# A hybrid SSM and attention encoder in fp32 on one core: another order of the first loads, zeros on TensorE, later lambda loads, four last pieces

## Chip, core and metric

The kernel runs on one core of one Trainium2 chip. The metric is the time of one execution on the device in microseconds; lower is better. Three runs of the kernel before took 1010.69 us in the median, from 1009.72 to 1019.44.

## What is computed

A residual stream x of 256 tokens by 2048 features passes a LayerNorm and then two layers. All is fp32.

```python
def reference(x, ...):
    x = layer_norm(x, ln_emb_g, ln_emb_b)
    for l in range(2):
        u, g_ssm, q, k, v, g_attn = split(x @ w_in[l])      # 2048 -> 6 x 1024
        y = u * ssm_d[l] + s5_scan(u, forward) + s5_scan(u, backward)
        y = gelu(y);  y = y * sigmoid(y @ w_glu[l] + b_glu[l]);  y_ssm = y * silu(g_ssm)
        lam = exp(sum(lambda_q1 * lambda_k1)) - exp(sum(lambda_q2 * lambda_k2)) + lambda_init
        o = rms_norm(diff_attention(rotary(q), rotary(k), v, lam), attn_norm_g[l])
        y_attn = o * (1 - lambda_init) * silu(g_attn)
        x = layer_norm(ALPHA * x + concat(y_ssm, y_attn) @ w_out[l], ln_g[l], ln_b[l])
    return x
```

`s5_scan` first makes small tables from `ssm_lam_re`, `ssm_lam_im` and `ssm_log_step` (exponentials, sines, a reciprocal), 64 groups by 64 states in each direction and layer.

## The kernel before

All weights stream through in tiles of 512 x 256, 512 KB each, in the order of the list `jobs`; I number them from 0. `load` (L144) asks for a tile on SP's DMA queue into one of four buffers `raw`. `do_split` (L156) makes two halves of it: ACT casts `raw` to `wh` (L163), DVE subtracts, `wl = raw - wh` (L165). A product of two fp32 numbers then is three matmuls on TensorE (PE), `mm3` (L168): high by high (L169), low by high (L170) and high by low (L171), with x split in the same way into `xh` and `xl`. A weight tile makes 8 x 3 = 24 matmuls of 256 columns. `step` (L863) splits two tiles ahead and loads four more ahead of these, then multiplies and lets `side` run other work.

The first eight weight tiles belong to two output blocks in turn (L889 to 895): for k tiles 0 to 3, then 4 to 7 and so on, one weight tile of each block. So weight tiles 0 to 3 multiply the first half of x's features, 4 to 7 the second half.

x goes through `ln_finish` (L213). It takes the moments of 128 tokens (`moments`, L220), normalises a piece of columns in two DVE passes (`centre` L230, `norm` L236), transposes it on PE into a `ss` bank (`trans`, L243), and makes `xh` by a cast on ACT (L253) and `xl` by a subtraction on DVE (L254). The pieces are k tiles 0-1, 2-3, 4-7, 8-11 and 12-15 (L281); the last two belong to weight tiles 4 to 7. Each normalised piece is also stored to `xres` for the residual addition (L211). The reciprocal root of the variance, `rstd`, is made on POOL in two steps (L224 adds epsilon, L225 is the power). After layer 1 the same function ends the kernel: there the second 128 tokens are done in the pieces of `LAST_PIECES`, and each is stored to the output (L241).

The start (L802 to L828): x is asked for in eight pieces, behind the first four the identity matrix (`cst`, L809) and the norm's rows `gt` and `bt` for the first 512 features (`load_gb`, L198), then the first four weight tiles with the other norm rows between them, then the other constants (L815).

Work beside the large products runs in lanes (`Lane`, `side`), which are generators: each `yield cost, gap` hands back and says after how many weight tiles it wants its next turn. `ssm_tables` (L296) loads its inputs (L303 to 306) and computes the tables in its first turns, `ssm_load` brings B and C and transposes them, `ssm_in` makes the SSM's input, `ssm_scan` scans it on DVE, `ssm_out` is its output. `lam_of` (L659) loads four lambda rows into the tile `on`, computes lambda, and loads `gsc` (L674), the gain of the headwise norm; it stands ahead of the first weight tile of a layer (L887). `on` is also used by the last table copies of `ssm_tables` and by the attention heads.

This order of calls is not the order on the engines. A scheduler (`schedule_with_timeline_sim=True`) simulates the program and writes each engine's instructions in the order in which they come out ready; the chip then works each engine's list strictly in that order. `with after(ins)` forbids it to place an instruction ahead of `ins`. In the program that comes out SP keeps eight DMAs under way: each issue waits until the one eight places ahead of it has landed.

## Time and profile before

| | before |
|---|---|
| median of three runs | 1010.69 us |
| the profiled execution | 1013.52 us |
| its span, first to last instruction | 1011.7 us |
| TensorE matmul (PE) busy | 960.5 us, 95% |
| weight load (PEld) | 928.7 us, 92% |
| VectorE (DVE) | 777.7 us, 77% |
| ScalarE (ACT) | 576.6 us, 57% |
| GpSimd (POOL) | 72.4 us, 7% |
| moved by DMA | 186.15 MB, 184 GB/s in the mean |

The span is what the profile shows from the first instruction to the last; about 2 us of the execution lie around it. Busy times are sums over the whole span, so they say nothing of a single stage. "PEclk" is the clock that TensorE was granted, as a share of its full 2.4 GHz: 1.00 is that, 0.50 is 1.2 GHz.

### The profile page before, as it was taken

What the parts mean: (1) busy time and instruction counts of PE and PEld (TensorE: products, weight loads), DVE (VectorE), ACT (ScalarE), POOL (GpSimd) and SP (SyncE); (2) the same over time, 40 slices, a digit from 0 to 9 for tenths busy, and PEclk for the clock granted to TensorE, in tenths of its full rate; (3) what the DMA queues carried; (4) which work ended last, traced back from release to release, by engine and by line L of the source; (5) the groups of instructions that cost most, each with busy time, mean ns of one, the idle gap of its engine ahead of it and who ended that gap; (6) DMA issues with size and microseconds to landing.
All of it is one profiled execution on the core that took longest, in us unless ns stands there. A gap on an engine that the chain in (4) does not pass through costs nothing.

```text
span 1011.7 us, 24655 instructions
## 1 busy us (share of the span) xinstructions
PE 960.5 (95%) x10304; PEld 928.7 (92%) x10304; DVE 777.7 (77%) x1326; ACT 576.6 (57%) x950; POOL 72.4 (7%) x103
## 2 busy tenths in 40 slices
PE   2899999999999998998889999999999999999995
PEld 2889988999999998998889989999999999999995
DVE  6784799899887696645489699989899759565576
ACT  2446588555575697435244486555556869833540
POOL 1000130110200000000001030010100100000001
PEclk9999999999999999999999999999999999999998
DMA  8897521545565644779974833555545454577883
GB/s 266 244 267 216 184 85 44 167 148 166 164 180 163 195 123 122 240 230 294 262 245 157 239 93 105 168 174 160 166 148 182 150 170 138 177 240 247 298 258 84
DMA packets 201871, 186.15 MB, mean 184 GB/s; under 512 B 38048, under 2 KB 194464, under 8 KB 201760
## 3 DMA queue, kind: packets, MB, share of 16 engines
q1 hardware_dynamic: 201760, 184.57, 60.1%
q8 instruction: 81, 1.33, 0.6%
q14 instruction: 30, 0.25, 0.1%
HBM read 169.21 MB, written 15.34 MB: 182 GB/s over the span
## 4 chain that ended last, share of the span: by engine, by line
PE 70%; DMA 13%; DVE 7%; ACT 4%; SPq 3%; issue 2%; POOL 1%; POOLq 0%; DVEq 0%; ACTq 0%
PE acc L169 19%; PE acc L170 19%; PE acc L171 19%; DMA rpart<-xr 5%; DMA raw<-in_w_out_dram 4%; DVE wl L165 2%; PE ss L502 2%; PE ss L597 2%; DMA raw<-in_w_glu_dram 2%; ACT wh L163 2%; PE tp L474 1%; PE sc L708 1%; PE ss L736 1%; SPq L428 1%; DVE H L236 1%
## 5 line engine op out<-in xcount | busy, mean ns | idle before, releaser
L165 DVE TENSOR_TENSOR wl<-raw,wh 128x1024 fp32r<-128x1024 f32 x266 | 324.7, 1222 | 148.4 <-ACT wh L163 146.6
L163 ACT CAST wh<-raw 128x1024 fp32r<-128x1024 f32 x266 | 278.4, 1050 | 265.7 <-PE acc L170 105.8
L169 PE MATMUL acc<-xh,wh 128*128 128x256 f32 x1280 | 370.7, 290 | 1.1 <-ACT xh L253 0.9
L170 PE MATMUL acc<-xl,wh 128*128 128x256 f32 x1280 | 365.4, 286 | 3.3 <-DVE xl L254 3.2
L171 PE MATMUL acc<-xh,wl 128*128 128x256 f32 x1280 | 364.3, 285 | 0.7 <-DVE wl L165 0.7
L169 PEld LDWEIGHTS acc<-xh,wh 128*128 128x128 f32 x1280 | 245.3, 192 | 6.1 <-ACT xh L253 1.6
L170 PEld LDWEIGHTS acc<-xl,wh 128*128 128x128 f32 x1280 | 245.8, 192 | 5.2 <-DVE xl L254 4.3
L171 PEld LDWEIGHTS acc<-xh,wl 128*128 128x128 f32 x1280 | 245.7, 192 | 1.8 <-DVE wl L165 1.1
L169 PE MATMUL acc<-wh,xh 128*128 128x256 f32 x720 | 206.0, 287 | 4.7 <-ACT wh L163 2.2
L170 PE MATMUL acc<-wl,xh 128*128 128x256 f32 x720 | 205.3, 286 | 2.4 <-DVE wl L165 1.7
L171 PE MATMUL acc<-wh,xl 128*128 128x256 f32 x720 | 204.1, 284 | 0.0
L169 PEld LDWEIGHTS acc<-wh,xh 128*128 128x128 f32 x720 | 138.5, 193 | 5.8 <-ACT wh L163 2.4
L170 PEld LDWEIGHTS acc<-wl,xh 128*128 128x128 f32 x720 | 138.5, 192 | 4.2 <-DVE wl L165 4.1
L171 PEld LDWEIGHTS acc<-wh,xl 128*128 128x128 f32 x720 | 138.4, 192 | 0.0
L552 DVE TENSOR_TENSOR sa<-tab,H 128x256 f32<-128x256 f32 x126 | 53.1, 421 | 2.9 <-ACT H L505 0.7
L459 DVE TENSOR_TENSOR w<-w,x 128x512 f32<-128x512 f32 x64 | 45.5, 711 | 0.8
L718 ACT ACTIVATE e<-sc,mx 128x256 f32<-128x256 f32 x64 | 29.5, 476 | 21.9 <-DVE mx L712 21.8
L555 DVE TENSOR_TENSOR H<-sa 128x128 f32<-128x128 f32 x126 | 36.1, 287 | 2.1
L554 DVE TENSOR_TENSOR sa<-sa,H 128x128 f32<-128x128 f32 x126 | 36.1, 286 | 1.9
L171 PE MATMUL acc<-bh,wl 128*128 128x256 f32 x128 | 36.4, 284 | 0.9 <-DVE wl L165 0.9
L742 POOL TENSOR_SCALAR ms<-ms 128x2 f32<-128x2 f32 x16 | 16.1, 1008 | 286.8 <-ACT on L741 286.8
L505 ACT COPY H<-ss 128x512 f32<-128x512 f32 x32 | 33.9, 1171 | 4.1 <-PE ss L502 4.1
(188 smaller groups left out, 1282.6 us busy)
## 6 DMA issues: line engine op xcount, KB each, us to landing
raw<-in_w_in_dram SPq DMA_DIRECT2D x192, 512.0 KB, 3.7
raw<-in_w_out_dram SPq DMA_DIRECT2D x64, 512.0 KB, 5.5
raw<-in_w_glu_dram SPq DMA_DIRECT2D x16, 512.0 KB, 5.9
xr<-xres SPq DMA_DIRECT2D x16, 256.0 KB, 3.2
rpart<-xr SPq DMA_DIRECT2D x16, 256.0 KB, 5.4
xr<-rpart SPq DMA_DIRECT2D x15, 256.0 KB, 4.4
xres<-H SPq DMA_DIRECT2D x14, 256.0 KB, 3.4
H<-in_x_dram SPq DMA_DIRECT2D x8, 256.0 KB, 5.9
```

The lines of the kernel that those rows point to most:

```text
L163: A.copy(wh, raw)
L165: V.tensor_tensor(wl, raw, wh.bitcast(F32), sub)
L169: PE.matmul(o, lhsT=lh, rhs=rh, start=first, stop=False, skip_group_check=True)
L170: PE.matmul(o, lhsT=lh, rhs=rl, start=False, stop=False, skip_group_check=True)
L171: PE.matmul(o, lhsT=ll, rhs=rh, start=False, stop=last, skip_group_check=True)
L459: V.tensor_tensor(w[:, r], w[:, r], x2, op)
L502: PE.matmul(ps[g2][ds, pr // 2, ri, pr % 2, :], lhsT=w[rows, pr, ds], rhs=u if d == 0 else u[:, ::-1], start=True, stop=True)
L505: A.copy(z.H[:, 2 * o:2 * o + 2, 1:65].rearrange("p q k r g -> p q (r g) k")[:, :, g2::2], ps[g2].rearrange("p q r g k -> p q (r g) k"))
L552: V.tensor_tensor(a.rearrange("p v q r g -> p v q (r g)"), lam, h.unsqueeze(1).to_broadcast([128, 2, 16, 8]), mult)
L554: V.tensor_tensor(a[:, 0], a[:, 0], nx, add)
L555: V.tensor_tensor(nx, a[:, 0], a[:, 1, :, ::-1, :], add)
L718: A.activation(e[:, m, i, :], sc[:, m, i, :], AF.Exp, bias=mx[:, c:c + 1], accum_out=sm[:, c:c + 1])
```

## The change

1. First loads. All of x is asked for, then the first norm rows, then weight tile 0. Weight tile 0's load is held until DVE has taken the statistics of the first 128 tokens (a memset of one element per partition of `raw`, ordered behind them). The other norm rows are ordered behind the newest weight load.
2. Zeros. A tile of zeros is made on POOL, and PE multiplies it ten times (`WARM`), 128 x 128 by 128 x 512, into a bank that is not read, ahead of the first transpose.
3. Start order. The first two splits name what they follow: the casts of weight tiles 0 and 1, and the `wl` behind the `xl` of their piece. The normalisation of a later piece also follows the `xl` before the last one.
4. SSM tables. Their loads are a turn of their own, the computation begins three weight tiles later (`TAB_HOP`), its first steps ordered behind the newest split.
5. Lambda. The loads of lambda and of `gsc` are a function `lam_load` that is called after the SSM input blocks, behind the newest weight load; `lam_of` computes from them after the first V block.
6. Tail. Epsilon is added on DVE, not on POOL. `LAST_PIECES` is (6,5,3,2), not (6,5,5). Each last piece's two stores are issued one from SP, one from ACT.

```diff
-LAST_PIECES = (6,5,5)
+LAST_PIECES = (6,5,3,2)
+WARM = 10
+TAB_HOP = 3
...
+    def load(i, hold=None):
...
+        if hold:
+            with after(hold):
+                V.memset(raw[:, 0, 0:1], 0.0)
...
-        A.copy(wh, raw)
-        with after(behind):
-            V.tensor_tensor(wl, raw, wh.bitcast(F32), sub)
+        with after(behind[0]):
+            newest[2] = A.copy(wh, raw).ins
+        with after(behind[1]):
+            newest[1] = V.tensor_tensor(wl, raw, wh.bitcast(F32), sub).ins
...
-            GP.tensor_scalar(rstd, mv[:, 1:2], EPS, None, add)
+            V.tensor_scalar(rstd, mv[:, 1:2], EPS, None, add)
...
-                for j in range(2):
-                    SY.dma_start(dst[2 * i + j][:, cs], r[64 * j:64 * j + 64, i, cs])
+                for j, eng in enumerate((SY, A)):
+                    eng.dma_start(dst[2 * i + j][:, cs], r[64 * j:64 * j + 64, i, cs])
...
-                with after(last):
+                with after(last), after(los[-2] if ahead < 8 and len(los) > 1 else None):
                     last = norm(i, k0, nk, *m)
...
+        yield 0.0, TAB_HOP
         step = T([128, 2], "p_st")
-        A.activation(step, ls, AF.Exp)
+        with after(newest[2]), after(newest[1]):
+            A.activation(step, ls, AF.Exp)
+        first = newest[1]
...
-    def lam_of(l):
+    def lam_load(l):
         t = T([128, 4, 64], "on")
...
+        gs = T([128, 1], "gsc", 2)
+        with after(newest[0]):
+            for i, src in enumerate((lambda_q1, lambda_k1, lambda_q2, lambda_k2)):
+                SY.dma_start(t[:, i, :], src[l:l + 1, :].to_broadcast([128, 64]))
+            SY.dma_start(gs, attn_norm_g[l].unsqueeze(1))
+        return t, gs
+
+    def lam_of(l, t, gs):
...
-            load_gb(gt, bt, ln_emb_g, ln_emb_b, slice(0, 512))
-    for c in range(RAW_BUFS):
-        load(c)
-        if c < 3:
-            load_gb(gt, bt, ln_emb_g, ln_emb_b, slice(512 * c + 512, 512 * c + 1024))
-    SY.dma_start(cst[:, C_SEL:], consts[:, C_SEL:])
+    load_gb(gt, bt, ln_emb_g, ln_emb_b, slice(0, 512))
+
+    idle = tp_bank([128, 512])
+    for _ in range(WARM):
+        PE.matmul(idle, lhsT=zero[:, 0:128], rhs=zero, start=True, stop=True)
...
+    for c in range(8):
+        seen = ln_stats(r, 0, c, st)
+    for c in range(RAW_BUFS):
+        load(c, hold=seen if c == 0 else None)
+        if c < 3:
+            with after(newest[0]):
+                load_gb(gt, bt, ln_emb_g, ln_emb_b, slice(512 * c + 512, 512 * c + 1024))
+    SY.dma_start(cst[:, C_SEL:], consts[:, C_SEL:])
+    next(ln)
+    for c in range(8):
+        ln_stats(r, 1, c, st)
     for i in range(SPLIT_AHEAD):
         next(ln)
-        do_split(i, behind=box[1][0])
+        do_split(i, behind=box[2] if i else (None, box[2][1]))
...
-        neg, gsc = lam_of(l)
...
+        lam = lam_load(l)
...
+                with after(newest[1]):
+                    neg, gsc = lam_of(l, *lam)
```

What stood in SP's queue behind the first four weight loads, before. `cst` are the constants, `on` the lambda rows, `kx` and `p_ls` the inputs of the SSM tables; the first `raw` is weight tile 4, the second tile 5:

```order
L815 DMA cst<-in_consts_dram 128x595
L662 DMA on<-in_lambda_q_dram 128x64
L662 DMA on<-in_lambda_k_dram 128x64
L662 DMA on<-in_lambda_q_dram 128x64
L662 DMA on<-in_lambda_k_dram 128x64
L150 DMA raw<-in_w_in_dram 128x4x256
L674 DMA gsc<-in_attn_norm_g_dram 128x1
L303 DMA kx<-in_ssm_lam_re_dram 64x2x64
L304 DMA kx<-in_ssm_lam_im_dram 64x2x64
L306 DMA p_ls<-in_ssm_log_step_dram 64x1
L150 DMA raw<-in_w_in_dram 128x4x256
```

In the changed kernel, from the last two table loads before weight tile 4 on; ahead of these stand the constants and the other table loads. The three `raw` of before and after are told apart by place: here the first is tile 4, the second tile 5.

```order
L313 DMA p_ls<-in_ssm_log_step_dram 64x1 x2
L310 DMA kx<-in_ssm_lam_re_dram 64x2x64
L311 DMA kx<-in_ssm_lam_im_dram 64x2x64
L313 DMA p_ls<-in_ssm_log_step_dram 64x1 x2
L155 DMA raw<-in_w_in_dram 128x4x256
L217 DMA xres<-H 128x512
L217 DMA xres<-H 128x256 x2
L217 DMA xres<-H 128x512
L448 DMA dd<-in_ssm_d_dram 16x16x1 x2
L217 DMA xres<-H 128x512
L448 DMA dd<-in_ssm_d_dram 16x16x1 x2
L155 DMA raw<-in_w_in_dram 128x4x256
```

Weight tile 4 stood between the lambda and the table loads; now it stands behind all table loads, and five stores of x and four small loads of `dd` stand between it and tile 5.

On ACT, before, from the cast of weight tile 3 on; `xh_117` is the first half of the features, `xh_141` the second:

```order
L163 CAST wh<-raw 128x1024
L253 CAST xh_117<-ss 128x512
L163 CAST wh<-raw 128x1024
L668 ACTIVATE le_178<-ls_176 128x2
L253 CAST xh_141<-ss 128x512
L308 ACTIVATE p_st<-p_ls 128x2
L163 CAST wh<-raw 128x1024
L253 CAST xh_141<-ss 128x512
L314 ACTIVATE kx<-kx 128x128
```

In the changed kernel, from the casts of weight tiles 1 and 2 on; `xh_131` is the first half, `xh_155` the second:

```order
L169 CAST wh<-raw 128x1024 x2
L260 CAST xh_131<-ss 128x512
L169 CAST wh<-raw 128x1024
L260 CAST xh_131<-ss 128x512
L169 CAST wh<-raw 128x1024 x2
L317 ACTIVATE p_st<-p_ls 128x2
L169 CAST wh<-raw 128x1024
L260 CAST xh_155<-ss 128x512 x2
L326 ACTIVATE kx<-kx 128x128
```

Before, the first cast of the second half stood behind the casts of weight tiles 3 and 4; now the casts of tiles 4, 5 and 6 stand ahead of it.

## Rows read from the trace of the kernel before

**Rows 1.** Stretches: from:to, length, busy of PE, PEld, DVE, ACT, POOL, PEclk, DMA, GB/s

```profile
0.00:20.00 20.00, 1.80 (x6) 1.01 (x6) 10.29 (x24) 3.10 (x4) 3.68 (x12) 1.00 0.91 261
...
40.00:60.00 20.00, 17.46 (x140) 16.65 (x139) 14.83 (x42) 9.91 (x14) 0.00 (x0) 1.00 0.88 261
...
140.00:160.00 20.00, 19.45 (x483) 16.16 (x471) 19.57 (x33) 15.77 (x28) 6.13 (x8) 1.00 0.10 30
```

**Rows 2.** PE's waits, 40 to 50 us: total, times, longest

```profile
PE acc L170 <- DVE xl L254: 2.3, 1, 2.3
```

**Rows 3.** Time line of ACT and DVE: start, busy, instruction, idle before and its releaser

```profile
16.03 1.04 ACT L163 CAST wh<-raw 128x1024 fp32r<-128x1024 f32 x1 [2.44 <-DMA raw<-in_w_in_dram]
...
18.95 1.22 DVE L165 TENSOR_TENSOR wl<-raw,wh 128x1024 fp32r<-128x1024 f32 x1
```

**Rows 4.** Time line of SP's queue: start and length of each DMA issue

```profile
17.24 0.33 SPq L815 DMA_DIRECT2D cst<-in_consts_dram  x1
...
22.98 0.38 SPq L150 DMA_DIRECT2D raw<-in_w_in_dram  x1
```

**Rows 5.** DMA issues at 17.24, from 25.5 to 28.4, and the stores of x

```profile
cst<-in_consts_dram SPq DMA_DIRECT2D x1, 297.5 KB, 8.8
...
raw<-in_w_in_dram SPq DMA_DIRECT2D x1, 512.0 KB, 3.6
...
DMA to landing us min/median/max: 3.2/4.7/5.2
```

**Rows 6.** Time line of PE: first matmuls of weight tiles 4 and 8

```profile
37.04 0.40 PE L169 MATMUL acc<-xh,wh 128*128 128x256 f32 x2
...
52.62 0.39 PE L169 MATMUL acc<-xh,wh 128*128 128x256 f32 x1 [0.18 <-ACT ub L881]
```

**Rows 7.** Time line of DVE from 36.35, and two later instructions

```profile
36.35 0.74 DVE L236 SCALAR_TENSOR_TENSOR H<-H,rstd 128x512 f32<-128x512 f32 x1
37.01 1.21 DVE L165 TENSOR_TENSOR wl<-raw,wh 128x1024 fp32r<-128x1024 f32 x1
38.15 0.68 DVE L254 TENSOR_TENSOR xl<-ss,xh 128x512 fp32r<-128x512 f32 x1
38.75 0.21 DVE L316 TENSOR_SCALAR kx<-kx 128x128 f32<-128x128 f32 x1
...
45.43 0.15 DVE L675 TENSOR_SCALAR gsc<-gsc 128x1 f32<-128x1 f32 x1 [5.00 <-DMA gsc<-in_attn_norm_g_dram]
...
52.26 0.94 DVE L340 RECIPROCAL kx<-kx 128x128 f32<-128x128 f32 x1
```

**Rows 8.** Stretches as in rows 1, a wait of PE, a group of matmuls

```profile
20.24:25.03 4.79, 4.66 (x20) 4.37 (x21) 4.79 (x8) 2.32 (x3) 0.00 (x0) 1.00 0.87 287
...
30.00:35.00 5.00, 5.00 (x44) 5.00 (x44) 5.00 (x8) 2.23 (x5) 0.00 (x0) 1.00 0.86 256
...
390.30:393.70 3.40, 3.40 (x86) 3.28 (x83) 2.37 (x4) 3.31 (x7) 0.00 (x0) 0.50 0.29 77
...
390.05 0.55 PE L597 MATMUL ss<-bh,w 64*64 64x64 f32 x8 [2.88 <-ACT ub L608]
...
L736 PE MATMUL ss<-v,wT 128*128 128x128 f32 x128 | 16.8, 274 | 0.0
```

**Rows 9.** PE's waits from 315 to 325 us

```profile
PE acc L171 <- DVE wl L165: 0.7, 1, 0.7
```

**Rows 10.** Time line of DVE at the end, and the stretch from 1009

```profile
1001.46 1.81 DVE L230 SCALAR_TENSOR_TENSOR H<-H,mv 128x768 f32<-128x768 f32 x2
...
1003.74 1.02 DVE L236 SCALAR_TENSOR_TENSOR H<-H,rstd 128x768 f32<-128x768 f32 x1 [0.47 <-POOL rstd L225]
...
1009.00:1010.00 1.00, 0.00 (x0) 0.00 (x0) 0.00 (x0) 0.00 (x0) 0.00 (x0) 0.50 1.01 261
```

**Rows 11.** The last step of the first layer's scan on DVE, and PE behind it

```profile
341.70 0.29 DVE L555 TENSOR_TENSOR H<-sa 128x128 f32<-128x128 f32 x1
...
349.47 0.69 PE L578 MATMUL tp<-cst,kw 128*64 128x64 f32 x16
```

More of the change, by code (lines that the diff above doesn't have):

```diff
@@ L141 @@
     raws, split = {}, {}
-    newest = [None]
-    def load(i):
+    newest = [None, None, None]
+    def load(i, hold=None):
         if i >= len(jobs):
@@ L154, in load, with do_split @@
         raws[i] = raw
-    def do_split(i, wh=None, wl=None, behind=None):
+    def do_split(i, wh=None, wl=None, behind=(None, None)):
         if i >= len(jobs):
@@ L201, in ln_stats @@
     def ln_stats(r, i, c, st):
-        V.bn_stats(st[:, i, c, :], r[:, i, c * 256:(c + 1) * 256])
+        return V.bn_stats(st[:, i, c, :], r[:, i, c * 256:(c + 1) * 256]).ins
     stores = []
@@ L218, in ln_finish @@
         pool = [None]
+        los = []
         def moments(i):
@@ L252, in trans @@
             h, lo_ = box[0].h[k0 // 8][sl], box[0].l[k0 // 8][sl]
-            A.copy(h, t)
-            V.tensor_tensor(lo_, t, h.bitcast(F32), sub)
+            box[2] = A.copy(h, t).ins, V.tensor_tensor(lo_, t, h.bitcast(F32), sub).ins
+            los.append(box[2][1])
         mv, rstd = moments(0)
@@ L306, in ssm_tables @@
                 SY.dma_start(ls[ps, d:d + 1], ssm_log_step[l, d].unsqueeze(1))
+        yield 0.0, TAB_HOP
         step = T([128, 2], "p_st")
-        A.activation(step, ls, AF.Exp)
+        with after(newest[2]), after(newest[1]):
+            A.activation(step, ls, AF.Exp)
+        first = newest[1]
         for d in range(2):
             dsl = slice(64 * d, 64 * d + 64)
-            V.tensor_scalar(zr[:, dsl], lr[:, dsl], step[:, d:d + 1], None, mult)
-            V.tensor_scalar(zi[:, dsl], li[:, dsl], step[:, d:d + 1], None, mult)
+            with after(first):
+                V.tensor_scalar(zr[:, dsl], lr[:, dsl], step[:, d:d + 1], None, mult)
+            with after(first):
+                V.tensor_scalar(zi[:, dsl], li[:, dsl], step[:, d:d + 1], None, mult)
         mag = t1
@@ L657 @@
     swap = list(range(8, 16)) + list(range(0, 8)) + list(range(16, 32))
-    def lam_of(l):
+    def lam_load(l):
         t = T([128, 4, 64], "on")
-        for i, src in enumerate((lambda_q1, lambda_k1, lambda_q2, lambda_k2)):
-            SY.dma_start(t[:, i, :], src[l:l + 1, :].to_broadcast([128, 64]))
+        gs = T([128, 1], "gsc", 2)
[5 more added lines that the diff above has]
+    def lam_of(l, t, gs):
         tv = t.rearrange("p (m k) d -> p m k d", m=2)
@@ L672, in lam_of @@
         V.scalar_tensor_tensor(neg, e2[:, 1:2], -init, e2[:, 0:1], add, sub)
-        gs = T([128, 1], "gsc", 2)
-        SY.dma_start(gs, attn_norm_g[l].unsqueeze(1))
         V.tensor_scalar(gs, gs, 1.0 - init, None, mult)
@@ L802 @@
     r, gt, bt = ln_tiles()
+    zero = T([128, 512], "e4")
+    GP.memset(zero, 0.0)
     for i in range(2):
@@ L818 @@
     ln = ln_finish(r, gt, bt, st, None, box, 4)
-    for i in range(2):
-        for c in range(8):
-            ln_stats(r, i, c, st)
-        if i == 0:
-            next(ln)
+    for c in range(8):
[9 more added lines that the diff above has]
+        ln_stats(r, 1, c, st)
     for i in range(SPLIT_AHEAD):
         next(ln)
-        do_split(i, behind=box[1][0])
+        do_split(i, behind=box[2] if i else (None, box[2][1]))
         load(RAW_BUFS + i)
```

## The prediction

> **What bounds the kernel now.** I read first the busy time by stretches, then PE's waits, then the queue of SP and the landing of its transfers, then DVE's instructions one by one. Up to about 20 us TensorE (PE) does next to nothing, 1.80 us in twenty; between 40 and 60 it loses another 2.5; from 60 on it loses little, 0.55 in the stretch from 140 to 160, one of the worse ones [rows 1]. So the kernel is bound by PE, and this change can only win what PE idles: the start, one wait at 44 us (2.3 us, for an `xl` that DVE is late with [rows 2]), small waits later, and the tail after PE's last matmul. The start itself is a matter of transfers and DVE: the first weight tile lands at 16.03, where ACT's wait for it ends, and its split is complete at 18.95 + 1.22 = 20.17 [rows 3]; PE's dense work begins there. I number the weight tiles from 0 in the order of `jobs`; tile 4 begins on PE at 37.04 and tile 8 at 52.62 [rows 6]. Up to tile 8 the change moves things; behind it PE sets the pace. So the first term is how much earlier or later tile 8 begins.
>
> **The start, up to the first matmul.** x is now asked for ahead of the first norm rows, so its second half lands earlier by about the 512 KB of these rows, 2 us at 261 GB/s [rows 1], and so do its statistics. That gain goes no further: ahead of weight tile 0 in the queue still stand all of x, the identity and the first norm rows, the same bytes, so it lands at 16.0 again or, with no gaps left (the share of the DMA engines was 0.91 up to 20 us [rows 1]), about 1.4 us earlier. ACT casts it before the first `xh`, `xl` waits for that, and the split follows `xl`: it ends between 19.1 and 20.2, against 20.17. Gain 0 to 1.1 us. The wait of tile 0 for the statistics (the memset on DVE) needs the first 1 MB of x, where 2.6 MB stand ahead of the tile in the queue: nothing.
>
> **Zeros on TensorE.** Before, the first 4.79 us of dense work hold 20 matmuls where 5.00 us later on hold 44 [rows 8]: half pace, 2.4 us lost. The ten zero matmuls would have to spare this. By the 0.27 us that 128 columns take [rows 8], times four, and twice that at half speed, they end at about 13; the first real matmul follows at 18. What PE does after such a pause the trace shows later: it sat idle from 387.17 to 390.05 and in 390.3 to 393.7 the granted clock was 0.50, that is 1.2 GHz for 2.4 [rows 8]. So I count the zeros at nothing; if the clock did hold, 2.4 us at most. They cost nothing either, since PE waits then; only if all ran at half speed, 10 x 2.2 = 22 us at most, would they stand before the first transposes. The Trainium skill (TensorE: Matmul & The Clock Gate, section "Part 1: The HAM clock gate") says that the throttled state is the default and that activity alone releases it, an idle engine falling back; the row at 390.3 agrees. By that rule the zeros gain nothing across the pause, which is what I take; without it the sum would be 2.4 us lower.
>
> **Table loads ahead of tile 4.** This is the term that decides. The scheduler put the eight small table loads directly behind the constants, and tile 4 behind them; before, tile 4 stood ahead of them and was issued at 22.98 [rows 4]. Eight transfers are under way at a time, each issue waiting for the one eight places ahead: so tile 4 waits for the first table load, which lands just behind the constants. These were issued at 17.24 and landed 8.8 us later, at 26.0 [rows 4, 5]; if the start's queue has fewer gaps now, 24. So tile 4 is issued at t4 = 24.3 to 26.7, I take 25.5, and lands 3.6 us later, as tile 5 did [rows 5]. Behind it now stand five stores of x and four small loads before tile 5, and tile 5 waits for the landing of the second store. A store takes 5.2 us from issue to landing, 3.2 at the least [rows 5]; the second is issued 1.0 behind tile 4 by my estimate, three issues of 0.33 [rows 4]. So tile 5 is issued at t4 + 6.0, tile 6 after the fourth store at about t4 + 7.0, and tile 6 lands at t4 + 10.6.
>
> Why tile 6 matters: ACT works in order, and the casts of tiles 5 and 6 now stand ahead of the first `xh` of k tiles 8 to 15, which tile 4 multiplies. After the landing come cast 1.05, split 1.14, `xl` 0.60 (the steps from one start to the next [rows 3, 7]) and about 0.1 between: 2.9 us. Tile 4 begins on PE at t4 + 13.5 = 39.0, against 37.04; with stores of 3.2 us and t4 24.3 at 36.3, with t4 26.7 at 40.2. PE waits some 3 us for it: its tiles 0 to 3 were through at 37.04 and begin 0 to 1.1 earlier now.
>
> **From tile 4 to tile 8.** Before, DVE stood 5.00 us at 45.43 for the small load of `gsc` that belongs to layer 1 [rows 7]. It goes. What is late next is DVE's own work: between the first `xl` for tile 4 and the first for tile 6 stand four passes of the normalisation at 0.66, one more `xl` 0.60, the split of tile 7 at 1.14, some twenty table steps of 0.13 to 0.3, a reciprocal of 0.9 [rows 7], the way of the sine over ACT, which I put at one more 0.9, and the `xl` itself: 2.6 + 0.6 + 1.1 + 4.1 + 0.9 + 0.9 = 10.2 us. PE needs 48 matmuls, 5.5 us, for tiles 4 and 5, and waits. Then the 46 matmuls behind that `xl` at 0.114 (44 in 5.00 us [rows 8]) are 5.2: tile 8 begins at 39.0 + 15.4 = 54.4, against 52.62, **1.8 us later**; bounds 51.7 and 55.6, that is -0.9 and +3.0, and 1.7 more if a stretch of half clock after the second wait falls on dense work.
>
> **Lambda later.** Besides the `gsc` load, layer 1's lambda loads go from the middle of the kernel, where DVE waited for them and PE 0.7 us for the split behind [rows 9]. They then land far ahead of their use: **-0.7**, bounds -0.9 and 0. In layer 0 the tile `on` is now held by lambda until tile 30, so the last table copies, and with them C's transposes and the SSM input, stand some three tiles later. PE does the same instructions; I take 0, bounds -1 and +2 (the rivals say where it could cost).
>
> **Tail.** The addition of epsilon leaves POOL. But beside POOL's two steps DVE does two centring passes of 1.81 in all, and only the 0.47 us up to 1003.74 were idle [rows 10]; DVE's own small addition takes 0.15 of that, as the one at 45.43 [rows 7]. The fourth piece adds two instructions of 0.1 each. The stores: the last microseconds move 261 GB/s at a share of 1.01 (the stretch from 1009 [rows 10]), so the engines are full with one queue; 1 MB needs 4.2 us whoever issues it. The first piece starts 0.3 earlier with both halves at once, and the last landing is of a smaller one: **-0.5**, bounds -1.1 and +0.2. The Trainium skill (DMA: Bandwidth & Descriptors, section "Issuing engines are not separate DMA queues") says that transfers issued from several engines run on the same 16 DMA engines and save issue time alone; the share of 1.01 agrees. Were the two queues two paths, half of the 4.2 us would go, and the sum would be 2.1 lower.
>
> **Sum.** +1.8 - 0.7 + 0 - 0.5 = +0.6 us. The profiled execution took 1013.5, so 1014.1 beside it; it stands 2.8 above the median of the runs shown, and on the scale of that median the forecast is 1010.7 + 0.6 = **1011.3 us**. Bounds added: -0.9 - 0.9 - 1 - 1.1 = -3.9 and +3.0 + 1.7 + 2 + 0.2 = +6.9, so 1006.8 to 1017.6. About 1% (10 us) is what a measurement of this kernel can tell from no change.
>
> **Rivals.** (a) The start works as the change says: stores land fast, tiles 5 and 6 arrive before DVE is ready, the clock holds. Then the wait of 2.3 at 44 us, the 2.4 of half clock and 1.1 at the first split go: -5.8 at tile 8, and with -0.7 and -0.5 the time is 1003.7. For it: PE's waits before were DVE's, not the queue's [rows 2]. Against: the order of SP and ACT, which no timing changes. (b) Slower: the SSM scan starts three tiles later in DVE's order and becomes the bound at its end. The scan's last step ended at 341.70 and the first matmul behind it began at 349.47 [rows 11], a reserve of 7.8 us; three tiles are 3 x 2.9 = 8.7 us. It decides once the scan ends more than 7.8 us later against PE than before. If DVE cannot catch up, and the SSM input, pressed into fewer tiles, leaves PE waiting for the same 8.7 us at 130 to 180 us, the time is 1011.3 + 8.7 = 1020.0. For it: DVE is busy for 19.57 of the 20 us from 140 on [rows 1]. Against: the order of the output stage has not moved, so the scheduler expects the lag to be made up. (c) The zeros do not do what they are for: they stay at half speed and hold up the first transposes by up to 4 us. The wait before tile 4 covers that; with 1 us not covered, 1012.3.
>
> **How the numbers follow.** Forecast 0.58, (a) 0.22, (b) 0.12, (c) 0.08. The range reaches from (a), 1004, to between the forecast's upper bound and (b), 1018; it leaves out half of (b) and the edges of (a). Faster by over 1% would need more than all of (a): 0.04. Slower by over 1% takes (b) and some of the upper bounds: 0.05. Within 1%: 0.91.
>
> **What would show it.** Tile 4's load issued at 24 to 27 on SP, tile 5's six us later; ACT idle for raw at 33 to 38; PE idle for some 3 us before the first matmul with the second half of `xh`, and again before tile 6; DVE without its 5.00 us for `gsc`; the last store's landing 0.5 us nearer to the last norm. Wrong would be: PE dense from 20 to 45 us without a wait (then (a)), or PE waiting for DVE between 130 and 180 us, or at 350 (then (b)).

## The result and the profile after

The changed kernel is slower: 1.0084 times the kernel before, with an interval of 1.0064 to 1.0104. On the scale of the median above, 1010.7 us, that is 1019.2 us (1017.2 to 1021.2). The forecast was 1011.3 with a range up to 1018.0. The time lies within 1%, as expected, but outside the range, and the loss is not the +0.6 us of the sum.

The profiled execution took 1017.46 us, with a span of 1015.7. It is one of the quicker runs of the changed kernel (the median of the fifteen that the ratio counts is 1019.53), so the profile shows 3.9 us of a loss of about 8.5. One run of the changed kernel, two of b_lambda and one of condition_alone took 2333 to 5134 us and count as slow; they are left out of every ratio here. Where the 3.9 us arise the profile shows. This table gives the begin of some weight tiles on PE, each read from its first matmul in the time line:

| begins at (us) | before | after | later by |
|---|---|---|---|
| tile 4 | 37.04 | 40.88 | +3.84 |
| tile 8 | 52.62 | 59.52 | +6.90 |
| tile 76 | 310.96 | 317.26 | +6.30 |
| tile 80 | 323.46 | 328.85 | +5.39 |
| last tile | 996.49 | 1001.53 | +5.04 |
| end of the span | 1011.74 | 1015.67 | +3.93 |

Up to tile 8 the change loses 6.9 us, and later it gains a little. The busy time by stretches of the changed kernel, in the columns of [rows 1], shows the same:

```profile
20.00:40.00 20.00, 15.46 (x112) 14.82 (x112) 14.31 (x22) 7.20 (x10) 0.00 (x0) 0.84 0.83 221
...
40.00:60.00 20.00, 16.89 (x111) 16.20 (x112) 17.82 (x51) 9.13 (x15) 0.00 (x0) 0.79 0.56 189
...
38.20:48.30 10.10, 6.85 (x30) 6.56 (x31) 9.24 (x24) 4.42 (x8) 0.00 (x0) 0.50 0.96 311
```

From 20 to 40 us PE is busy for 15.46 us, where it was 19.18 in that stretch before; and from 38.2 to 48.3 the granted clock is 0.50, 1.2 GHz, where it was 1.00. PE's waits from 30 to 60 us (total, times, longest) replace the one of [rows 2]:

```profile
PE acc L175 <- ACT xh L260: 4.8, 1, 4.8
...
PE acc L176 <- DVE xl L260: 2.2, 2, 1.7
```

The wait of 4.8 us is in front of tile 4, for an `xh`, that is for ACT. ACT's time line, the counterpart of [rows 3], shows the casts of tiles 4, 5 and 6 and behind them the first casts of the second half:

```profile
30.12 1.05 ACT L169 CAST wh<-raw 128x1024 fp32r<-128x1024 f32 x1 [2.52 <-DVE xl L260]
...
37.03 1.04 ACT L169 CAST wh<-raw 128x1024 fp32r<-128x1024 f32 x1 [5.85 <-DMA raw<-in_w_in_dram]
...
39.29 1.04 ACT L169 CAST wh<-raw 128x1024 fp32r<-128x1024 f32 x1 [1.11 <-DMA raw<-in_w_in_dram]
...
40.24 1.07 ACT L260 CAST xh<-ss 128x512 fp32r<-128x512 f32 x2
```

ACT is idle for 5.85 us for tile 5's load and 1.11 for tile 6's, and only then makes `xh` (L260). Here are the issues in SP's queue [rows 4] and the landing of tile 6, issued at 33.72 [rows 5]:

```profile
25.92 0.52 SPq L155 DMA_DIRECT2D raw<-in_w_in_dram  x1
...
32.24 0.39 SPq L155 DMA_DIRECT2D raw<-in_w_in_dram  x1
...
33.72 0.52 SPq L155 DMA_DIRECT2D raw<-in_w_in_dram  x1
...
raw<-in_w_in_dram SPq DMA_DIRECT2D x1, 512.0 KB, 5.5
```

Some links of the chain of waits (start, length, what), in order of time:

```profile
33.72 5.47 DMA raw<-in_w_in_dram
...
39.29 1.05 ACT wh L169
...
40.37 1.22 DVE wl L171
...
41.59 0.61 DVE xl L260
...
42.25 0.58 PE acc L176
...
43.05 0.21 PE acc L175
...
49.32 1.06 ACT wh L169
...
50.40 1.23 DVE wl L171
...
52.03 0.86 DVE kx L352
...
52.89 0.56 DVE xl L260
```

It runs from tile 6's load over its cast, its split and the `xl` to PE, then along PE at 0.21 us a matmul, half pace; then from the end of tile 4's products back to ACT, which needs its buffer `wh` for the cast of tile 7, to that tile's split, a reciprocal of the tables, and the `xl` of tile 6. At full clock the steps are 0.12. From 42.25 to 48.4 the half clock so costs 6.15 x (1 - 0.12 / 0.21), some 2.6 us by this estimate. These are the first matmuls of tiles 4 and 8 [rows 6]:

```profile
40.88 0.80 PE L175 MATMUL acc<-xh,wh 128*128 128x256 f32 x2 [4.82 <-ACT xh L260]
...
59.52 0.39 PE L175 MATMUL acc<-xh,wh 128*128 128x256 f32 x1
```

The end of the scan on DVE and the first matmul behind it [rows 11]:

```profile
354.51 0.29 DVE L567 TENSOR_TENSOR H<-sa 128x128 f32<-128x128 f32 x1
...
354.86 0.69 PE L590 MATMUL tp<-cst,kw 128*64 128x64 f32 x16
```

The reserve, 7.8 us from the begin of the scan's last step or 7.5 from its end, is used up: PE takes the result at 354.86, 0.06 behind the scan's end (354.51 + 0.29). The last norm [rows 10]:

```profile
1006.31 1.80 DVE L237 SCALAR_TENSOR_TENSOR H<-H,mv 128x768 f32<-128x768 f32 x2
...
1008.03 1.01 DVE L243 SCALAR_TENSOR_TENSOR H<-H,rstd 128x768 f32<-128x768 f32 x1
```

No wait stands between the centring and the first piece now.

### The profile page after: what moved, and what is told of

It is laid out like the page before. It is cut to its first block, busy times and chain, and to the rows that moved or that the text cites. A ratio compares the mean times of both kernels' runs of the same rounds, so it can differ in the third digit from the quotient of the medians.

```text
span 1015.7 us, 24716 instructions
## 1 busy us (share of the span) xinstructions
PE 967.7 (95%) x10324; PEld 933.1 (92%) x10324; DVE 781.5 (77%) x1335; ACT 574.7 (57%) x948; POOL 61.1 (6%) x98
## 4 chain that ended last, share of the span: by engine, by line
PE 75%; DMA 9%; DVE 9%; ACT 2%; SPq 2%; issue 1%; POOL 0%; DVEq 0%; ACTq 0%
PE acc L175 22%; PE acc L176 22%; PE acc L177 21%; DMA raw<-in_w_out_dram 3%; DMA raw<-in_w_in_dram 2%; PE ss L609 2%; DVE wl L171 2%; PE ss L752 1%; PE sc L724 1%; DVE w L469 1%; ACT wh L169 1%; DVE x L469 1%; DVE w L471 1%; DMA a<-y_dr 1%; PE tp L590 1%
## 5 line engine op out<-in xcount | busy, mean ns | idle before, releaser
L175 PEld LDWEIGHTS acc<-xh,wh 128*128 128x128 f32 x1280 | 248.0, 194 | 11.8 <-ACT xh L260 7.7
L651 ACT COPY bh<-H 128x1024 f32<-128x1024 f32 x16 | 34.7, 2181 | 1.9 <-DVE H L567 1.1
```

The lines of the kernel that those rows point to most:

```text
L175: PE.matmul(o, lhsT=lh, rhs=rh, start=first, stop=False, skip_group_check=True)
L651: A.copy(hc, src)
```

## Experiments

All runs at a glance, with the begin of three weight tiles and the end of the span in the profile, and the time as a ratio to the kernel before. Labels that begin with b_, and condition_alone, are the kernel before with something added; the others are the changed kernel with something altered.

| run | tile 4 | tile 8 | last tile | end | ratio to before (interval) |
|---|---|---|---|---|---|
| before | 37.04 | 52.62 | 996.5 | 1011.7 | 1 |
| changed | 40.88 | 59.52 | 1001.5 | 1015.7 | 1.0084 (1.0064 to 1.0104) |
| no_zeros | 37.79 | 61.45 | 1007.1 | 1021.4 | 1.0106 (1.0065 to 1.0147) |
| xh_first | 36.58 | 54.35 | 999.4 | 1013.7 | 1.0026 (1.0002 to 1.0051) |
| all_behind | 37.93 | 55.65 | 1001.0 | 1015.3 | 1.0059 (1.0032 to 1.0086) |
| bridge | 41.77 | 62.74 | 1005.7 | 1019.9 | 1.0157 (1.0095 to 1.0219) |
| fix | 36.64 | 54.36 | 1001.1 | 1015.4 | 1.0042 (1.0019 to 1.0065) |
| fix_nozeros | 37.27 | 53.63 | 996.9 | 1011.2 | 1.0030 (1.0011 to 1.0049) |
| norm_only | 35.95 | 49.65 | 995.4 | 1009.7 | 1.0001 (0.9978 to 1.0024) |
| zeros14 | 39.94 | 59.13 | 1008.4 | 1022.8 | 1.0056 (1.0034 to 1.0078) |
| b_tail | 37.66 | 50.99 | 998.0 | 1012.2 | 0.9992 (0.9974 to 1.0010) |
| b_lambda | 36.98 | 49.70 | 995.0 | 1010.2 | 0.9983 (0.9964 to 1.0001) |
| b_lambda_tail | 36.70 | 49.42 | 988.4 | 1002.7 | 0.9970 (0.9949 to 0.9992) |
| b_xfirst | 39.77 | 53.39 | 995.5 | 1010.0 | 0.9987 (0.9968 to 1.0005) |
| condition_alone | 35.92 | 56.84 | 995.0 | 1009.3 | 1.0011 (0.9993 to 1.0028) |

The spans are of single executions, which scatter by several microseconds, much of it where transfers set the pace (tiles 96 to 132 and from 252 on); that of b_lambda_tail is the quickest of its twelve, 1004.51 us where their median is 1010.57. So tile 4 and tile 8 are read from the profile, the time as a whole from the ratio. Tile 8 scatters too: before and b_tail, whose orders on every engine are the same up to there, differ by 1.6 us at it.

**The order on ACT (xh_first).** My theory after the first reading: `xh` is late because of where it stands on ACT.

```diff
     def step(fn, budget=BUDGET):
...
-        do_split(ji + SPLIT_AHEAD)
+        do_split(ji + SPLIT_AHEAD, behind=(box[2][0] if ji == 3 else None, None))
```

> The changed kernel, with ACT's cast of weight tile 5 held behind the first two casts of x's second half, so that these wait for weight tile 4 alone and not for tiles 5 and 6; SP's order stays. My theory: the wait before tile 4 (4.8 us) comes from that order on ACT. It goes: tile 4 begins at 35.5 to 37.5 instead of 40.9, the half clock from 38 to 48 us does not come, and tile 8 begins at 52 to 56 instead of 59.5. Rival: the late landings of tiles 5 and 6 or DVE's table steps hold PE all the same, now in front of tile 5: tile 8 begins behind 57.

Measured: tile 4 at 36.58, no half clock between 25 and 144 us, tile 8 at 54.35. The theory holds: 5.2 of the 6.9 us are gone, and the time falls from 1.0084 to 1.0026 (the intervals lie apart). What remains is in front of tile 6 and of tile 8, in PE's time line:

```profile
45.00 0.88 PE L256 MATMUL ss<-cst,H 128*128 128x128 f32 x6 [1.57 <-DVE H L243]
...
46.22 0.39 PE L175 MATMUL acc<-xh,wh 128*128 128x256 f32 x1 [0.35 <-ACT xh L260]
...
54.15 0.27 PE L387 MATMUL tp<-cst,a 64*128 64x64 f32 x1 [1.10 <-DVE a L359]
```

The transposes of the last piece wait for DVE's normalisation (1.57), and the table transposes for the tables (1.10).

**The queue (all_behind).** The forecast had put the blame on SP's queue. This run orders what stood ahead of tiles 4 to 6 behind them.

```diff
-            SY.dma_start(lr[ps]...
+            with after(newest[0]):
+                SY.dma_start(lr[ps]...
...
-                SY.dma_start(*stores.pop(0))
+                with after(newest[0]):
+                    SY.dma_start(*stores.pop(0))
```

(and likewise the other table loads and `dd`.)

> The changed kernel, with table loads, stores of x and the small loads of dd ordered behind the newest weight load; ACT's order stays (casts of tiles 4, 5 and 6 ahead of the second half). My theory: the queue on SP is the origin. Tiles 4 to 6 are issued by 28 us, tile 6 lands by 33, tile 4 begins at 35 to 37, no half clock from 38 on, tile 8 at 51 to 55; the time is 4 to 8 us below the changed kernel's, within 0.4% of the kernel before. Rival: DVE's order (normalisation and table steps between the first and the third product of the second half) sets the pace: tile 8 behind 57, the time within 2 us of the changed kernel's.

Measured: the loads come as meant, tile 6 is issued at 27.23 and lands at 32.29, 6.9 earlier; but tile 4 begins at 37.93 and tile 8 at 55.65. PE waits 0.8 us for an `xh` and 2.8 in two waits for `xl`, and from 40.2 to 47.0 the granted clock is 0.75 in the mean, where no half clock was expected. ACT's time line shows what is late in the queue's place:

```profile
30.36 1.05 ACT L169 CAST wh<-raw 128x1024 fp32r<-128x1024 f32 x1 [1.74 <-PE acc L176]
...
34.80 1.05 ACT L169 CAST wh<-raw 128x1024 fp32r<-128x1024 f32 x1 [3.39 <-PE acc L176]
...
36.34 1.05 ACT L169 CAST wh<-raw 128x1024 fp32r<-128x1024 f32 x1 [0.40 <-PE acc L176]
...
37.30 1.06 ACT L261 CAST xh<-ss 128x512 fp32r<-128x512 f32 x2
```

The casts of tiles 5 and 6 now wait for PE (3.39 and 0.40): there are three buffers `wh`, so tile 6 can be cast only when PE is through with tile 3. The first `xh` of the second half (37.30) stands behind that cast, so it comes when PE has run out of tiles 0 to 3, however early the data is there. The expectation, tile 4 at 35 to 37 and tile 8 at 51 to 55, was missed by 0.9 and 0.65, and the time lies 0.25% below the changed kernel's, which is not told apart from nothing, where 4 to 8 us were expected. So mending the queue alone does not undo the loss.

**Both (fix).** The edits of the two runs above together.

> The changed kernel with both repairs of the start: loads of weight tiles 4 to 6 ahead of table loads and stores, and ACT's cast of tile 5 behind the first two casts of the second half. Theory: then nothing of the 6.9 us is left: tile 8 begins at 50 to 54 us, and the time stands 0 to 2 us below that of the kernel with the ACT order alone (0.3% above the kernel before), so within 0.3% of the kernel before. Rival: DVE's order holds the third product of the second half, and tile 8 stays at 54 to 56.

Measured: tile 8 at 54.36, as with the ACT order alone (54.35). So the queue adds nothing here once ACT's order is mended, and the rival is right: PE's waits are those of xh_first again, 1.53 us for DVE's normalisation and 1.10 for the tables. The time, 1.0042, is not below that of xh_first (1.0026), as the theory had it, and not told apart from it.

**One condition (norm_only).** What put ACT and DVE into that order? The candidate is the condition that a piece's normalisation also follows the `xl` before the last one. The edit takes it out and leaves all the rest of the change:

```diff
-                with after(last), after(los[-2] if ahead < 8 and len(los) > 1 else None):
+                with after(last):
```

> The changed kernel with one condition less: a piece's normalisation no longer has to follow the xl before the last one. That alone puts ACT's first cast of the second half back ahead of the casts of tiles 5 and 6, and DVE's passes for the last piece ahead of the splits of tiles 4 and 5. Theory: this one condition is the origin of the 6.9 us at weight tile 8. Tile 4 begins at 35.5 to 37.5, no wait over 1 us in front of tile 6, tile 8 begins at 49 to 51.5 (52.62 before), and the time lies 0.1 to 0.5% below the kernel before. Rival: the delayed tables or the loads behind each other hold tile 6 all the same, and tile 8 begins behind 53, as with the ACT order alone (54.35).

Measured: tile 4 at 35.95, tile 8 at 49.65, that is 9.9 us earlier than in the changed kernel by this one line. ACT's time line, then PE's waits from 30 to 60 us, then the stretch that was at half clock:

```profile
30.02 1.05 ACT L169 CAST wh<-raw 128x1024 fp32r<-128x1024 f32 x1 [2.11 <-DMA raw<-in_w_in_dram]
...
31.52 0.59 ACT L260 CAST xh<-ss 128x512 fp32r<-128x512 f32 x1 [0.45 <-PE ss L256]
...
36.69 1.05 ACT L169 CAST wh<-raw 128x1024 fp32r<-128x1024 f32 x1 [4.58 <-DMA raw<-in_w_in_dram]
...
37.75 0.56 ACT L260 CAST xh<-ss 128x512 fp32r<-128x512 f32 x1
```

```profile
PE acc L177 <- DVE wl L171: 0.3, 1, 0.3
...
PE acc L175 <- ACT ub L904: 0.2, 1, 0.2
```

```profile
38.20:48.30 10.10, 9.73 (x79) 9.44 (x79) 9.18 (x24) 6.75 (x12) 0.00 (x0) 1.00 1.01 296
```

The first `xh` (31.52) stands right behind tile 4's cast again, ahead of tile 5's, though tiles 5 and 6 land at 36.59 and 38.02, hardly earlier than in the changed kernel (36.93 and 39.19). ACT waits 4.58 us for tile 5, and PE waits for none of it. The condition acts through the pieces: without it PE transposes the first piece of the second half at 30.89, with it at 33.70 and 35.24. That this is why the scheduler places the casts of tiles 5 and 6 first is argued, not shown. PE waits for nothing worth the name, and the clock is at 1.00. The time falls from 1.0084 to 1.0001, so the whole slowdown goes with the condition. The scheduler built the rest of the start anew as well (tile 5's load is issued at 28.91 instead of 32.24), so the 9.9 us are those of the whole order that the condition forces, DVE's passes included, not of ACT's casts alone. That it stops at "no change" rather than 0.1 to 0.5% below was not expected. Its profile loses 3.0 us at 950 us in a wait for ACT, which had itself been idle 4.84 us for a load of `w_out`; in the other profiles the same wait is between nothing and 2.0. Whether this is only the scatter of transfers stays open.

**The condition alone.** Is it enough by itself? Here it stands on the kernel before with lambda and tail, without the new order of loads, the zeros or the later tables.

```diff
+        los = []
...
-                with after(last):
+                with after(last), after(los[-2] if ahead < 8 and len(los) > 1 else None):
```

> The kernel before with lambda and tail, and of the rest of the change that one condition alone (a piece's normalisation also follows the xl before the last one). Theory: the condition is enough by itself. It puts ACT's cast of tile 5 ahead of the second half's first cast, and DVE's passes for the last piece behind the splits of tiles 5 and 6, as in the changed kernel; tile 8 begins at 52 to 57 us instead of 49.4, and the time lies 0.3 to 0.8% above that of the kernel without it (0.9970 of the kernel before). Rival: it costs only together with the changed order of loads and the later tables; tile 8 begins at 49 to 51, and the time is within 0.2% of 0.9970.

Measured: tile 8 at 56.84 against 49.42, and 1.0011 against 0.9970: enough by itself for a loss of 0.4%, half of the changed kernel's 0.83% (the intervals only just lie apart, 0.9993 against 0.9992). PE's waits from 30 to 60 us, rows of ACT, and the stretch behind:

```profile
PE acc L169 <- ACT xh L254: 2.4, 1, 2.4
...
PE acc L170 <- DVE xl L255: 2.3, 2, 1.3
```

```profile
33.92 1.05 ACT L163 CAST wh<-raw 128x1024 fp32r<-128x1024 f32 x1 [3.39 <-PE acc L170]
...
35.20 1.07 ACT L254 CAST xh<-ss 128x512 fp32r<-128x512 f32 x2
...
44.47 1.03 ACT L163 CAST wh<-raw 128x1024 fp32r<-128x1024 f32 x1
...
45.71 1.05 ACT L254 CAST xh<-ss 128x512 fp32r<-128x512 f32 x2
```

```profile
47.10:53.90 6.80, 5.75 (x27) 5.75 (x28) 6.66 (x25) 0.00 (x0) 0.00 (x0) 0.50 0.39 130
```

Again tile 5's cast waits for PE (3.39) with the first `xh` behind it, but that costs little here: tile 4 begins at 35.92, earlier than without the condition (36.70). Most of the loss lies in front of tile 6 and behind it: the `xh` of the last piece (45.71), whose transposes end at 43.92, stands on ACT behind steps of the sine and the cast of tile 8 (44.47); PE waits 2.4 us for it and 1.3 for its `xl`, and then the clock is at 0.50 for 6.8 us. So it is ACT's order again, but at another place than in the changed kernel.

**The pause and the clock (bridge).** Four more zero matmuls behind tile 3 were to fill PE's wait (`mmlast` is the newest product).

```diff
+            if l == 0 and s == 1:
+                idle = tp_bank([128, 512])
+                for _ in range(4):
+                    with after(mmlast[0]):
+                        PE.matmul(idle, lhsT=zero[:, 0:128], rhs=zero, start=True, stop=True)
```

> The changed kernel with four more zero matmuls on PE between weight tiles 3 and 4, where it waits for 4.8 us; they write a bank that nothing reads. My theory: that pause is what drops the clock to half from 38 to 48 us, and this costs 3.1 us. With the pause filled the granted clock stays at 1.00, tile 4 begins at 40.5 to 42 as before, and tile 8 at 55.5 to 57.5 instead of 59.5. Rival: the clock falls all the same, or DVE holds tile 6: tile 8 begins at 59 to 60.

Measured: tile 8 at 62.74. The time line of PE and the stretch behind:

```profile
35.34 3.60 PE L924 MATMUL tp<-e 128*128 128x512 f32 x8
...
41.77 0.80 PE L176 MATMUL acc<-xh,wh 128*128 128x256 f32 x2 [2.18 <-ACT xh L261]
...
44.56 0.58 PE L177 MATMUL acc<-xl,wh 128*128 128x256 f32 x1 [2.00 <-DVE xl L261]
```

```profile
41.70:48.40 6.70, 4.63 (x20) 4.34 (x21) 6.56 (x21) 2.70 (x6) 0.00 (x0) 0.50 0.84 282
```

The zeros were through before the `xh` came; pauses of 2.18 and 2.00 stayed, and the clock fell all the same, as the rival had it, with tile 8 later than either side expected. The pause was not filled, so the run does not tell the theories apart. The half clock at this place goes with the pause in front of tile 4: xh_first and norm_only have neither. That the pause is its cause is argued from that and not shown by a run that fills it.

**The zeros (no_zeros, fix_nozeros, zeros14).** The first is the changed kernel, the second is fix, the third is xh_first, each with one number changed.

```diff
-WARM = 10
+WARM = 0
```

(in zeros14: `WARM = 14`.)

> The changed kernel without the ten zero matmuls. My theory: they play no part in the 6.9 us that tile 8 is late; they fill PE while it waits anyway, and the clock falls again behind them. Tile 8 begins at 58 to 61 us (59.5 with the zeros), the time stays within 2 us of the changed kernel's, 0.6 to 1.0% above the kernel before. Rival: the zeros cost or gain something themselves. If they cost, tile 8 begins before 57 and the time falls by over 2 us; if they gain, tile 8 begins behind 61 and the time rises by over 2 us.

Measured: tiles 1 to 3 begin 0.1 us later than with zeros (tile 1 at 26.43 against 26.31). Tile 4 comes earlier and tile 8 later: 61.45 and 1.0106 are outside the theory and by the letter what the rival gave for zeros that gain. But the scheduler, without the zeros, chose another order on SP, ACT and DVE, and the intervals of the two times overlap. So the total does not speak for or against the zeros, the first tiles do.

> The same without the ten zero matmuls. Theory: the zeros are worth nothing, since the granted clock falls to half at about 17 us behind them and rises at 24 to 25 with and without them: weight tiles 0 to 3 begin within 0.3 us of the kernel with zeros. Rival: they hold the clock for the first products: tiles 1 to 3 begin 0.5 us or more later without them.

Measured: tile 1 at 27.19 against 26.54, tile 8 at 53.63 against 54.36, the time 1.0030 against 1.0042, which is not told apart. At the first tiles the rival's 0.5 us is reached, at tile 8 nothing of it is left. Between 0.1 and 0.65 us at tile 1 is what ten zeros bring in these single executions; before and b_tail, with the same order, differ by 0.28 there.

> The changed kernel with the ACT order repaired (as xh_first), and fourteen zero matmuls instead of ten, which reach to about 18 us, close to the first real product. Theory: the ten zeros were worth nothing because PE paused behind them. With the pause gone the granted clock stays at 1.00 from 7 us on, and tile 1 begins 2 to 4 us earlier than with ten (26.49), at 22.5 to 24.5, or as early as its split allows. Rival: the clock falls at 17 to 18 all the same, whatever PE does; tile 1 begins at 26.5 or later.

Measured: the clock (two stretches) and what tile 1 waits for:

```profile
18.00:21.20 3.20, 1.09 (x4) 0.69 (x5) 2.92 (x6) 0.52 (x2) 0.00 (x0) 1.00 1.06 366
...
21.30:24.60 3.30, 3.05 (x15) 2.65 (x14) 3.09 (x5) 1.06 (x2) 0.00 (x0) 0.50 0.89 281
...
24.89 2.36 DVE L171 TENSOR_TENSOR wl<-raw,wh 128x1024 fp32r<-128x1024 f32 x2 [0.43 <-ACT wh L169]
...
26.52 0.36 PE L175 MATMUL acc<-xh,wh 128*128 128x256 f32 x1
```

With the pause shortened the clock stays at 1.00 up to 21.3, where it had fallen at 17.7 in the changed kernel. But tile 1 begins at 26.52, unchanged (26.49 in xh_first): up to 21.2 PE had 1.09 us of work, and behind it the clock was at 0.50 for 3.3 us of nearly dense work. The split of tile 1 ends only at 26.1 (the row from 24.89 holds those of tiles 1 and 2), so its products with `wl` could not have come before that in any case. What a clock at 1.00 throughout would bring is not shown. In this kernel the order on ACT and DVE is that of xh_first, but the scheduler put tile 4's load behind two stores and four small loads, at 31.24 instead of 25.25, and tile 8 slipped from 54.35 to 59.13: so the queue can cost nearly as much as ACT's order did, once it holds tile 4 itself.

**The parts that gain (b_lambda, b_tail, b_lambda_tail, b_xfirst).** Their edits are parts 5 and 6 of the change, word for word, one, the other and both (epsilon on DVE in the last norm alone); b_xfirst has both and this:

```diff
         if i == 0:
             SY.dma_start(cst[:, 0:C_SEL], consts[:, 0:C_SEL])
-            load_gb(gt, bt, ln_emb_g, ln_emb_b, slice(0, 512))
+    load_gb(gt, bt, ln_emb_g, ln_emb_b, slice(0, 512))
```

> The kernel before with the lambda and gsc loads moved alone (no tail, no zeros, no change of the start's loads, no delay of the tables). ACT keeps the second half's first cast behind weight tile 4 alone. Theory: the move itself is a gain. The wait of 2.3 us before weight tile 6 goes, tile 8 begins at 50 to 52.6 us (52.62 before), 0.9 us go at layer 1's tile 80, and the scan, which starts later, uses its reserve up without becoming the bound: the time is 0.1 to 0.4% below the kernel before. Rival: the later scan and tables cost it: PE waits for the scan at 350 us or behind it, and the time is 0.1 to 0.4% above.

Measured: tile 8 at 49.70, 2.9 earlier than before and 1.3 earlier than in b_tail, tile 80 another 0.9, and 0.9983. Both tiles come out on the theory's side, tile 8 even earlier than its 50 to 52.6; the time agrees but is not told apart from 1 (0.9964 to 1.0001).

> The kernel before with the tail alone: epsilon of the last norm added on DVE, four last pieces, each one's two stores issued from SP and from ACT. Theory: this is worth the 1.1 us that the changed kernel's profile gained between the last weight tile and the end of the span (5.04 later on PE, 3.93 later at the end). So 0.8 to 1.3 us between PE's last weight tile and the end, and a time 0 to 0.2% below the kernel before. Rival, from the full DMA engines: half of it or nothing, 0 to 0.5 us.

Measured: last tile 1.54 later than before and end 0.50 later, in that execution, so 1.04 us gained behind the last tile. The time, 0.9992, agrees but cannot be told from 1.

> The kernel before with the lambda move and the tail, nothing else of the change. Theory: the two gains add, since they lie at different ends: 2.9 us less at tile 8, 0.9 at layer 1's tile 80, 1.0 to 1.1 behind the last weight tile; the time is 0.2 to 0.5% below the kernel before. Rival: what is gained at tile 8 is lost again where transfers set the pace, and only the tail is left, 0.1%.

Measured: 0.9970 (0.9949 to 0.9992), the best kernel of the study, some 3 us below the kernel before, and 1.1% below the changed one.

> The kernel before with lambda, tail, and all of x asked for ahead of the first norm rows (no zeros, no hold, no named order of the splits). Theory: the order of the loads by itself is worth at most 1.4 us at the first split, and nothing once tile 4 is reached; tile 4 begins at 35.6 to 37, the time is within 0.2% of the kernel with lambda and tail alone. Rival: it is a loss or a gain of its own of more than 2 us at tile 8, by the order that the scheduler then finds on ACT and DVE.

Measured: asking for all of x first lets tile 1 begin at 25.00 (25.22 in b_lambda_tail), but the scheduler then builds an order in which PE waits 3.0 us within tile 2, and tile 8 begins at 53.39, 4.0 later than without. The theory's tile 4 (35.6 to 37) is missed, at 39.77, and the rival holds for tile 8; the time, 0.9987, is 0.17% above that of b_lambda_tail and not told apart from it.

## Why the prediction was wrong

- **Table loads ahead of tile 4**, "the term that decides", and with it the +1.8 us at tile 8: this step failed. Measured were +6.90 us. Its order of events was right: tile 4 was issued at 25.92 (25.5 forecast), tile 5 at 32.24 (t4 + 6.0 = 31.9), tile 6 at 33.72 (t4 + 7.0 = 32.9). But the lock is not the queue by itself. The prediction said that ACT works in order and that the casts of tiles 5 and 6 stand ahead of the first `xh`, and took it as a path for the queue's delay. Mending ACT's order gained 0.6%, and dropping the condition that made this order all 0.83%, 9.9 us at tile 8, with the loads of tiles 5 and 6 landing nearly as late; mending the queue gained 0.25%, which is not told apart from nothing. The condition was read (it is in the list of the change) and was given no term.
- The signs that the prediction named came true: tile 4's issue, tile 5's six microseconds later, ACT idle for `raw`, PE idle in front of tile 4. They follow from either cause, so they could not tell the queue from the condition.
- The size: tile 6 landed 5.5 us behind its issue instead of 3.6, so tile 4 began at 40.88, against 39.0 and an upper bound of 40.2. It would have been later still, had the way from the landing to tile 4 taken the 2.9 us of the prediction; it took 1.7 (39.19 to 40.88), since the first product needs `xh` alone and not the split and the `xl`.
- **From tile 4 to tile 8** it was to take 15.4 us and took 18.64. The work of DVE between the first `xl` for tile 4 and the first for tile 6 was put at 10.2 us and took 11.3 (41.51 to 52.81), but what held it was not DVE's passes alone: the split of tile 7 among them waited for PE to free a buffer at half clock. The stretch of half clock was in the bounds with 1.7 us; it lasted 10 us, where the row it was taken from shows 3.40, and cost some 2.6. The Trainium skill (TensorE: Matmul & The Clock Gate, section "Part 1: The HAM clock gate") says that an idle engine falls back to the slow state; the trace agrees, 4.82 us of waiting and then 0.50 up to 48.4.
- What carried the time out of the range is only in part this profile: its +3.9 us would give 1014.6, inside the range. The rest is the larger loss of the other executions; it goes with the condition too, since norm_only is back at 1.0001.
- The sums: with stores of 3.2 us and tile 4 issued at 24.3, tile 4 begins at 24.3 + 11.5 = 35.8, not 36.3; the 10.2 us leave out the `xl` that their list ends with, 0.6; and 1 MB at 261 GB/s are 4.0 us, not 4.2. None of it decides.
- **Zeros on TensorE**, counted at nothing, was right: the clock fell to 0.50 at 17.7 behind them, and tiles 1 to 3 moved by 0.1 to 0.65 us. The reason given, the pause, was only half of it: with the clock held up to 21.3 (zeros14) tile 1 did not begin earlier. As for the half pace before that the zeros were to spare: in 20.24 to 25.03 the row of [rows 8] prints 1.00, but the matmuls of the trace stand 0.21 us apart there, as at 0.50 elsewhere.
- **The start**: tile 0 landed 1.2 us earlier (14.82), but ACT loaded its table only then, 1.28 us from 14.89 on, and the first split ended at 20.29 against 20.17, so nothing was gained there. Tile 3 began 1.6 us earlier, more than the 1.1 allowed, and it was worth nothing at tile 4.
- **Lambda later**, forecast -0.7, measured -0.91 at tile 80. In layer 0 I took 0; b_lambda shows -2.9 at tile 8 against the profile before and -1.3 against b_tail, whose order is the same as before: DVE's wait for `gsc` goes, and nothing takes its place in an order without the condition. The prediction had let other work take it.
- **Tail**, forecast -0.5, measured -1.11, the bound. Of it 0.24 is DVE's last norm, 0.61 between DVE's last instruction and the end; the rest lies ahead of the last statistics. The two queues, the pieces and epsilon were not tried apart.
- Rival (b), the scan that starts later, came true up to its threshold: the reserve was used up to 0.06 us, and PE was 5.39 late at tile 84 and 6.10 at tile 92, so 0.7 at most are its price. It did not decide. Of rival (a)'s -5.8 at tile 8 norm_only shows half, -3.0: without the condition PE does run on through the start.

The sum of the profile is 6.9 at tile 8, -0.6 up to tile 76, -0.9 for lambda, -0.35 up to the last tile, -1.1 in the tail: +3.9. The larger loss in the median of the runs is not traced. The record points at the clock: over its span the profiled run was granted 0.983 in the mean, as much as any of the fifteen, whose median is 0.980. On 1016 us that difference is some 6 us more at 0.50, and costs 3 us at most (an estimate: half of the 6). It would not be all of the missing 4.6.

## What to carry to other kernels

An ordering condition that costs nothing where it is written can turn the order on engines that it does not name: here a condition on DVE's normalisation moved two casts on ACT ahead of the one that PE was waiting for, and cost 9.9 us at tile 8, with DVE's own new order. After such an edit, read the order of each engine and ask of every instruction ahead of the late one what it waits for itself: a load, or, through a ring of buffers, the very engine that waits. And when several edits come together, measure them one at a time: two of these six parts gain together 0.3%, and one condition of a third loses more than they bring. The first loads (beyond asking for x first), the rest of part 3 and the later tables were not measured alone; the kernel with all of them and without the condition stands at 1.0001, the kernel without any of them at 0.9970, and these intervals overlap.

## What the runs showed of the hardware

- The granted clock fell behind waits of PE in the start stage and stayed at 0.50 for some time after PE had resumed its work: through the 10.1 us shown of the changed kernel, the 6.7 of bridge, the 6.8 of condition_alone and the 3.3 of zeros14. In zeros14 the fall at 21.3 came behind three pauses of only 0.73, 0.79 and 0.74 us.
- The ten zero matmuls of 512 columns in fp32 took 11.41 us from 2.25 us on, 1.14 each, and the clock records of that profile begin at 7.4 us with 1.00.
- The small load of `gsc`, 0.5 KB, held DVE for 5.00 us in the profile before and for 2.70 in b_tail, whose order up to there is the same; there PE's wait of 2.3 us is gone. So this wait is large or small from one execution to the next.
